# One more tile of lead for the weight parts in the up projection of a hybrid decoder trunk

## The chip, the core and the metric

The kernel runs on one core of a Trainium2 chip. The metric is device time in microseconds (us) of one execution of the whole program. TensorE (PE in the profile, PEld for its weight loads), VectorE (DVE), ScalarE (ACT), GpSimd (POOL) and SyncE (SP, which here only issues DMAs) each run their own instruction list in order and wait for one another by semaphores.

## The reference, cut to what matters

The reference is one layer of a decoder trunk on 256 rows of width 2048 in float32: an RMSNorm, a combined input projection, two token mixers, an output projection, a residual, and then a gated MLP. Only the MLP's first product is touched by the change:

```python
h = rmsnorm(x, norm_ffn_w[l])
gate, up = jnp.split(jnp.einsum('bsd,df->bsf', h, w_up[l]), 2, axis=-1)
gate = causal_dwconv(gate, conv_ffn_w[l]) + conv_ffn_b[l]
x = x + jnp.einsum('bsf,fd->bsd', jax.nn.gelu(gate, approximate=False) * up, w_down[l])
```

`w_up` is 2048 x 11264 (gate and up, 5632 columns each), so the product is 256 x 2048 by 2048 x 11264.

## The kernel before, in words

**Weights come as tiles.** The whole program walks through one list of weight tiles, `srcs`, each 256 rows x 512 columns of a matrix, held in SBUF as 128 partitions x 2 x 512 float32 (512 KB). For each tile three steps are made before TensorE uses it: a DMA into a buffer with the tag `raw` (`load_part`, L203); on ACT a cast of it to the rounded type float32r, the high part `whi` (L289); on DVE the difference of the two, the low part `wlo` (L297, called the split here). TensorE then multiplies high by high, high by low and low by high. `begin(n)` (L277) asks for cast and split of all tiles up to n; `weights()` (L197) is called once for each tile just before its matmuls and calls `begin(taken + AHEAD + 1)` with AHEAD = 2. So while tile n is multiplied, the cast and split of tile n+2 are asked for. `raw` has four buffers; `whi` and `wlo` have three each (the pool's `bufs=3`, L62). A cast of tile n therefore waits until TensorE has made its last use of the high part of tile n-3, a split until it has used up the low part of tile n-3, and a load of a raw tile until the split of the raw tile four places back is done.

**The up projection goes in groups.** There are 11 groups c = 0 to 10 of 512 gate and 512 up columns. Most of the depth of a group is done "plain": one tile, twelve matmuls of 512 columns. For a part of it the kernel uses a scheme with seven products in place of eight. The depth of 2048 is cut into four chunks of 512; a chunk treated so gives seven "parts", named T1, 11, T2, 21, T3, 22, T4, each with six matmuls. Groups 1 to 7 and 9 (`TWO`, L96) treat two chunks, 1 and 0, so they have 14 parts and 8 plain tiles; groups 8 and 10 treat one. The parts of group c+1 are put between and behind the last plain tiles of group c, so that a stretch from one group to the next is: four gate tiles and one up tile in a row, then T1, up, 11, up, T1, 11, up, and then ten parts in a row (T2, T2, 21, 21, T3, T3, 22, 22, T4, T4), with the transposes of the finished gate ahead of T3 and those of the finished up ahead of T4. `up_steps` (L100 to L127) lists this, and the PE instructions keep that order exactly (`manual_schedule`, L1446).

**Parts need sums.** A chunk's four raw quarters are loaded by `quad_load` (L218) into buffers `quad` that belong to other tags (`xt0` to `xt3`, `hhi6` to `hlo9`). Three of the seven parts are quarters themselves; the four T parts are made on DVE by subtraction in place (`up_sum`, L225, profile line L230): T1 = 12 - 11, T2 = 22 - T1 and so on, so a buffer gets its next sum only after the part in it has been cast and split. `sums_behind` says behind which tile's split each sum is put; the first T1 of a group is asked for in the main loop at `n - 3 == i` (L1482), three steps ahead of the entry that marks where the parts begin. The quarters are asked for 5 to 13 steps ahead of that entry (L1478).

**Beside the weights**, DVE also adds two pairs of products in PSUM per group (L1396, L1410), and for the group just finished makes the causal convolution (eight instructions, L1331), the product of gate and up (L1344) and the low part of the result (L1352). ACT does their activations (L1326, L1335), copies out of PSUM (L1403, L1407, L1424, L1427) and the cast L1351.

**The order on the other engines.** Outside the lists fixed by hand, a planner orders each engine's instructions: what is traced earlier in the program has the higher priority, and among the ready ones (by the planner's own estimate of times) the first is taken. On the chip each engine then runs its list in that order. `issue_after` puts an instruction behind another of its engine. The SP list holds all weight and quarter loads of this stage.

The tag `s` of the pool `fp` is a single buffer of 128 x 1024 float32; it holds sums of activations at the start of the stage (`four_sums`, L1279) and again from group 10 on.

Of the kernel before, what the change touches and what calls it, by code (L numbers as in the profile page):

```python
# [35 lines left out]
def kernel(  # L36
# [32 lines left out]
    def nm(s):  # L69
        cnt[0] += 1  # L70
        return f"{s}_{cnt[0]}"
# [30 lines left out]
    for c in range(NUP):  # L102
        kps = [kp for kp in range(KD // 2) if kp // 2 not in chunks_of[c]]
        gate_steps, up_only = ([("plain", c, col, kp) for kp in kps] for col in range(2))
        tail = min(6, len(kps)) if c + 1 in TWO else TAIL
        up_steps += gate_steps[:tail]
        for a, b in zip(gate_steps[tail:], up_only):
            up_steps += [a, b]
        rest = up_only[-tail:]
        if c + 1 == NUP:  # L110
            up_steps += rest
            break
        parts = [[("part", c + 1, what, ch) for what in UP_PARTS] for ch in chunks_of[c + 1]]
        if len(rest) == 4:
            up_steps += [rest.pop(0)]
        up_steps += [("loads", c + 1)]
        if c + 1 in TWO:
            first_four = [parts[ch][n] for ch in range(2) for n in (0, 1)] + [parts[ch][2] for ch in range(2)]
            if len(rest) == 3:
                rest = rest[:2] + [None] + rest[2:] + [None, None]  # L120
            for a, b in zip(first_four, rest):
                up_steps += [a, b] if b else [a]
            p21, t3, p22, t4 = ([parts[ch][n] for ch in range(2)] for n in range(3, 7))
            up_steps += p21 + [("gate", c)] + t3 + p22 + [("up", c)] + t4
        else:
            t1, p11, t2, p21, t3, p22, t4 = parts[0]
            up_steps += [t1, rest[0], p11, rest[1], t2, rest[2], p21, ("gate", c), t3, p22, ("up", c), t4]  # L127
    for step in up_steps:
        if step[0] == "plain":
            srcs.append(up_w[step[1]][step[2]][step[3]])  # L130
        elif step[0] == "part":
            srcs.append(("up", *step[1:]))
# [55 lines left out]
    made = []  # L188
    taken = [0]

    loads = []
    last_load = [None]
    last_split = [None]
# [2 lines left out]

    def weights(ahead=AHEAD):  # L197

        begin(taken[0] + ahead + 1)
        taken[0] += 1  # L200
        return made[taken[0] - 1]

    def load_part(n, k):  # L203
        if n == len(loads):
            if isinstance(srcs[n], tuple):
                loads.append(quarter(*srcs[n]))
                return
            loads.append(wpool.tile(list(srcs[n].shape), F32, tag="raw", name=nm("raw"), bufs=4))
        last_load[0] = nc.sync.dma_start(loads[n][:, k], srcs[n][:, k]).ins

    quarters = {}
# [65 lines left out]
    def begin(n):  # L277
        while len(made) < min(len(srcs), n):
            load(len(made) + 1)
            raw = loads[len(made)]  # L280
            if isinstance(raw, tuple):
                raw, plus, minus = raw
                nc.vector.tensor_tensor(raw, plus, minus, op=ALU.subtract)
            src = srcs[len(made)]
            shape = list(raw.shape)
            keep = kept.get(len(made))
            hi = wpool.tile(shape, F32R, tag="whi", name=nm("whi")) if keep is None else \
                mtile(keep, shape, F32R, nm("khi"))
            nc.scalar.copy(hi, raw)  # L289
            if shape[1] == 8:  # L290
                lo = None
                nc.vector.tensor_tensor(hi[:, :, 32:64], raw[:, :, 0:32], hi[:, :, 0:32].bitcast(F32),
                                        op=ALU.subtract)
            else:
                lo = wpool.tile(shape, F32R, tag="wlo", name=nm("wlo")) if keep is None else \
                    mtile(4 + keep, shape, F32R, nm("klo"))
                last_split[0] = nc.vector.tensor_tensor(lo, raw, hi.bitcast(F32), op=ALU.subtract).ins  # L297
                splits.append(last_split[0])
            made.append((hi, lo))
            for more in sums_behind.get(len(made) - 1, ()):  # L300
                up_sum(*more)
            if isinstance(src, tuple) and src[0] != "up" and src[2] in ("T1", "T3", "T2", "T4"):
                next_quarter()
# [94 lines left out]
    def mtile(i, shape, dt, name):  # L398
        return big.tile(shape, dt, tag=f"m{i}", name=name)
# [1047 lines left out]
    for i, step in enumerate(up_steps):  # L1447
# [28 lines left out]
        for n, step in enumerate(up_steps):  # L1476
            if step[0] == "loads":
                when = (7, 7, 6, 5, 13, 12, 11, 10) if step[1] in TWO else (8, 7, 6, 5)  # L1478
                for q in sorted(range(len(when)), key=lambda q: -when[q]):
                    if max(n - when[q], 0) == i:  # L1480
                        quad_load(step[1], q)
                if n - 3 == i:  # L1482
                    up_sum(step[1], "T1", chunks_of[step[1]][0])
    pe_order.close()

# [192 lines left out]
```

## Time and profile before

| what | value |
|---|---|
| median of three runs | 1541.56 us (1541.18 to 1541.80) |
| the profiled execution: its own time, and its span from first to last instruction | 1542.63 us, 1540.8 us |
| PE busy over the span | 1526.0 us (99%) |
| DVE, ACT busy over the span | 1253.4 us (81%), 849.8 us (55%) |
| first and last matmul of the up projection's tiles | 819 us, 1299 us after the span's start |
| granted TensorE clock | 0.999 |

A row of a timeline or a group has start (or count), duration, engine, the line in the kernel, the operation, and output<-inputs; in square brackets stands how long the engine had been idle before it and what released it. A row of the waits has the total, the number of waits and the longest. A row of windows has the length of the stretch and each engine's busy time in it, with the number of instructions in brackets.

### The profile page before, as it was taken

What the parts mean: (1) busy time and instruction counts of PE and PEld (TensorE: products, weight loads), DVE (VectorE), ACT (ScalarE), POOL (GpSimd) and SP (SyncE); (2) the same over time, 40 slices, a digit from 0 to 9 for tenths busy, and PEclk for the clock granted to TensorE, in tenths of its full rate; (3) what the DMA queues carried; (4) which work ended last, traced back from release to release, by engine and by line L of the source; (5) the groups of instructions that cost most, each with busy time, mean ns of one, the idle gap of its engine ahead of it and who ended that gap; (6) DMA issues with size and microseconds to landing.
All of it is one profiled execution on the core that took longest, in us unless ns stands there. A gap on an engine that the chain in (4) does not pass through costs nothing.

```text
span 1540.8 us, 20209 instructions
## 1 busy us (share of the span) xinstructions
PE 1526.0 (99%) x7302; PEld 1257.4 (82%) x7302; DVE 1253.4 (81%) x1776; ACT 849.8 (55%) x1063; POOL 70.8 (5%) x90
## 2 busy tenths in 40 slices
PE   9999999999999999999999999999999999999998
PEld 8887888788878888788888888888788888888886
DVE  6788859896589858987667899999999886878885
ACT  7455446454455445454455676666667665555552
POOL 1010002000100000000000000000000000000100
PEclk9999999999999999999999999999999999999999
DMA  8776757776577766776578646666457467556652
GB/s 276 215 221 199 202 163 214 213 214 183 152 245 205 205 169 201 222 200 186 179 250 300 194 163 217 219 205 205 150 155 242 125 216 267 183 193 205 227 189 90
DMA packets 166674, 310.46 MB, mean 201 GB/s; under 512 B 19458, under 2 KB 23330, under 8 KB 166446
## 3 DMA queue, kind: packets, MB, share of 16 engines
q1 hardware_dynamic: 159456, 287.37, 60.0%
q0 software_dynamic: 5184, 18.88, 3.7%
q10 hardware_dynamic: 1934, 2.93, 0.5%
q8 instruction: 57, 0.93, 0.2%
q14 instruction: 43, 0.35, 0.1%
HBM read 301.75 MB, written 7.38 MB: 201 GB/s over the span
## 4 chain that ended last, share of the span: by engine, by line
PE 92%; DVE 4%; issue 2%; DMA 1%; ACT 0%; POOL 0%; POOLq 0%; DVEq 0%; ACTq 0%
PE psg L1374 25%; PE psm L334 15%; PE psm L332 14%; PE psm L333 14%; PE psm L1359 7%; PE psg L1359 7%; DVE wlo L297 3%; PE psm L1374 2%; PE psm L478 1%; PE psg L377 1%; DVE quad L230 1%; PE psm L1436 1%; DMA vrow<-ev 1%; PE psg L868 1%; DMA mv<-vrow 1%
## 5 line engine op out<-in xcount | busy, mean ns | idle before, releaser
L289 ACT CAST whi<-raw 128x1024 fp32r<-128x1024 f32 x428 | 450.0, 1052 | 428.4 <-PE psm L333 280.2
L297 DVE TENSOR_TENSOR wlo<-raw,whi 128x1024 fp32r<-128x1024 f32 x426 | 517.3, 1220 | 151.2 <-ACT whi L289 146.2
L289 ACT CAST whi<-quad 128x1024 fp32r<-128x1024 f32 x168 | 176.1, 1054 | 141.0 <-DVE quad L230 39.4
L297 DVE TENSOR_TENSOR wlo<-quad,whi 128x1024 fp32r<-128x1024 f32 x168 | 202.6, 1219 | 36.2 <-ACT whi L289 35.3
L334 PE MATMUL psm<-wlo,xhl 128*128 128x512 f32 x432 | 169.5, 393 | 1.6 <-DVE wlo L297 1.6
L332 PE MATMUL psm<-whi,xhl 128*128 128x512 f32 x432 | 169.0, 391 | 0.0
L333 PE MATMUL psm<-whi,xhl 128*128 128x512 f32 x432 | 168.6, 390 | 0.0
L1374 PE MATMUL psg<-whi,fhl 128*128 128x512 f32 x504 | 127.1, 389 | 0.0
L1374 PEld LDWEIGHTS psg<-whi,fhl 128*128 128x128 f32 x504 | 94.4, 188 | 19.5
L334 PEld LDWEIGHTS psm<-wlo,xhl 128*128 128x128 f32 x432 | 81.1, 188 | 19.0 <-DVE wlo L297 2.4
L333 PEld LDWEIGHTS psm<-whi,xhl 128*128 128x128 f32 x432 | 81.1, 188 | 16.8
L332 PEld LDWEIGHTS psm<-whi,xhl 128*128 128x128 f32 x432 | 81.1, 188 | 16.6
L230 DVE TENSOR_TENSOR quad<-quad,quad 128x1024 f32<-128x1024 f32 x72 | 87.6, 1217 | 0.0
L1374 PE MATMUL psg<-wlo,fhl 128*128 128x512 f32 x252 | 69.9, 389 | 0.0
L1374 PE MATMUL psg<-whi,ups 128*128 128x512 f32 x216 | 58.9, 394 | 0.0
L1359 PE MATMUL psm<-whi,hhi 128*128 128x512 f32 (+1 forms) x150 | 58.1, 387 | 0.0
L1359 PE MATMUL psm<-whi,hlo 128*128 128x512 f32 (+1 forms) x150 | 57.9, 386 | 0.0
L1359 PE MATMUL psm<-wlo,hhi 128*128 128x512 f32 (+1 forms) x150 | 57.4, 387 | 0.1
L1374 PEld LDWEIGHTS psg<-wlo,fhl 128*128 128x128 f32 x252 | 47.3, 188 | 9.8
L332 PE MATMUL psm<-whi,mhi 128*128 128x512 f32 x128 | 50.8, 397 | 0.0
L1359 PE MATMUL psg<-whi,hhi 128*128 128x512 f32 (+1 forms) x130 | 50.3, 387 | 0.4 <-ACT whi L289 0.4
L1359 PE MATMUL psg<-whi,hlo 128*128 128x512 f32 (+1 forms) x130 | 50.0, 386 | 0.0
(432 smaller groups left out, 2927.3 us busy)
## 6 DMA issues: line engine op xcount, KB each, us to landing
raw<-in_w_in_dram SPq DMA_DIRECT2D x224, 512.0 KB, 4.2
raw<-in_w_up_dram SPq DMA_DIRECT2D x104, 512.0 KB, 4.8
quad<-in_w_up_dram SPq DMA_DIRECT2D x72, 512.0 KB, 4.9
raw<-in_w_down_dram SPq DMA_DIRECT2D x64, 512.0 KB, 4.7
raw<-in_w_out_dram SPq DMA_DIRECT2D x32, 512.0 KB, 4.2
quad<-in_w_down_dram POOLq DMA_DIRECT2D x24, 512.0 KB, 5.5
mv<-vrow SPq DMA_DIRECT2D x12, 512.0 KB, 4.9
taps<-in_conv_qkv_w_dram SPq DMA_DIRECT2D x16, 256.0 KB, 6.8
```

The source lines that it names most:

```text
L230: nc.vector.tensor_tensor(out_, plus_, minus_, op=ALU.subtract)
L289: nc.scalar.copy(hi, raw)
L297: last_split[0] = nc.vector.tensor_tensor(lo, raw, hi.bitcast(F32), op=ALU.subtract).ins
L332: mm(ps[:, t, :], lh(k, t), hi[:, kk, :], start=(k == 0), stop=False)
L333: mm(ps[:, t, :], ll(k, t), hi[:, kk, :], start=False, stop=False)
L334: mm(ps[:, t, :], lh(k, t), lo[:, kk, :], start=False, stop=(k == nk - 1))
L377: nc.tensor.transpose(pt[:, ff, t * P : (t + 1) * P], src[:, t, f * P : (f + 1) * P], ident)
L478: mm(ps_k0[:, t, :], part(k, t), w[:, kk, :], start=(k == 0 and w is hi and part is xh), stop=(k == KD - 1 and w is lo))
L868: mm(pg0, kq[:, h, 0, 0:P], kq[:, h, :, :], start=True, stop=True)
L1359: mm(ps[:, cs], lhs(kk), part_[:, kk, cs], start=(first and kk == 0 and n == 0), stop=(last and kk == 1 and n == 2), skip_group_check=shared)
L1374: mm(ps, lhs(kk), w[n][:, kk], start=(first and n == 0 and kk == 0 and lhs is high), stop=False, skip_group_check=True)
L1436: nc.tensor.transpose(out_[f // 2][:, f % 2, t * P : (t + 1) * P], e[:, t, f * P : (f + 1) * P], ident)
```

## The change

From the first part of group 1 to the last part of group 9 (the "deep" stretch, tiles 10 to 202 of the up projection, counted from 0) each tile's cast and split are asked for three tiles ahead instead of two. For this, every fourth tile of the stretch gets its high part in a new buffer `spare` and its low part in the buffer with tag `s`; the other three of four keep using the three `whi` and `wlo` buffers, which now come round every fourth tile. `spare` is what was the fourth `raw` buffer: `raw` has three buffers now, and outside the stretch every fourth raw tile is loaded into `spare`, so there are four again there. The first T1 sum of a group is asked for one step earlier for groups up to 9. Nothing is computed differently, and no instruction is added or removed.

```diff
+    deep = [0, 0]
     for step in up_steps:
+        if step[0] == "part" and not deep[0]:
+            deep[0] = len(srcs)
+        if step[0] == "part" and step[1] < NUP - 1:
+            deep[1] = len(srcs) + 1
...
+    plain_loads = [0]
...
     def weights(ahead=AHEAD):

-        begin(taken[0] + ahead + 1)
+        begin(taken[0] + ahead + (2 if deep[0] <= taken[0] + ahead + 1 < deep[1] else 1))
...
-            loads.append(wpool.tile(list(srcs[n].shape), F32, tag="raw", name=nm("raw"), bufs=4))
+            spare = not deep[0] <= n < deep[1] and plain_loads[0] % 4 == 3
+            loads.append(wpool.tile(list(srcs[n].shape), F32, tag="spare" if spare else "raw", name=nm("raw"),
+                                    bufs=1 if spare else 3))
+            plain_loads[0] += 1
+            if deep[0] <= n + 1 < deep[1]:
+                plain_loads[0] = 0
...
-            hi = wpool.tile(shape, F32R, tag="whi", name=nm("whi")) if keep is None else \
-                mtile(keep, shape, F32R, nm("khi"))
+            fourth = deep[0] <= len(made) < deep[1] and (len(made) - deep[0]) % 4 == 3
+            if fourth:
+                hi = wpool.tile(shape, F32R, tag="spare", name=nm("whi"), bufs=1)
+            else:
+                hi = wpool.tile(shape, F32R, tag="whi", name=nm("whi")) if keep is None else \
+                    mtile(keep, shape, F32R, nm("khi"))
...
-                lo = wpool.tile(shape, F32R, tag="wlo", name=nm("wlo")) if keep is None else \
-                    mtile(4 + keep, shape, F32R, nm("klo"))
+                if fourth:
+                    lo = fp.tile(shape, F32R, tag="s", name=nm("wlo"))
+                else:
+                    lo = wpool.tile(shape, F32R, tag="wlo", name=nm("wlo")) if keep is None else \
+                        mtile(4 + keep, shape, F32R, nm("klo"))
...
-                if n - 3 == i:
+                if n - (4 if step[1] < NUP - 1 else 3) == i:
                     up_sum(step[1], "T1", chunks_of[step[1]][0])
```

## The prediction

> **What bounds the kernel now.** I read the page first, then the waits of PE and PEld, then the windows from one stall to the next, and last the timelines around a stall. The page's first line, then the waits of PE and of PEld over the up projection (819 to 1300 us):
>
> ```profile
> PE 1526.0 (99%) x7302; PEld 1257.4 (82%) x7302; DVE 1253.4 (81%) x1776; ACT 849.8 (55%) x1063; POOL 70.8 (5%) x90
> ...
> PE psg L1374 <- DVE wlo L297: 4.0, 7, 0.6
> ...
> PEld psg L1374 <- DVE wlo L297: 7.1, 8, 1.1
> ```
>
> TensorE bounds the kernel, and in the up projection it waits for one thing only: seven times for a low part. The timelines of PE, then DVE, then ACT, around the last of the seven:
>
> ```profile
> 1129.11 1.07 PE L1374 MATMUL psg<-wlo,fhl 128*128 128x512 f32 x4
> 1130.02 1.07 PE L1374 MATMUL psg<-whi,ups 128*128 128x512 f32 x4
> ...
> 1135.01 0.63 PE L1374 MATMUL psg<-wlo,fhl 128*128 128x512 f32 x2
> ...
> 1139.08 1.07 PE L1374 MATMUL psg<-whi,ups 128*128 128x512 f32 x4
> 1139.99 0.63 PE L1374 MATMUL psg<-wlo,ups 128*128 128x512 f32 x2
> 1140.46 1.08 PE L1374 MATMUL psg<-whi,ups 128*128 128x512 f32 x4
> 1142.14 0.73 PE L1374 MATMUL psg<-wlo,ups 128*128 128x512 f32 x2 [0.60 <-DVE wlo L297]
> ```
> ```profile
> 1132.31 1.23 DVE L297 TENSOR_TENSOR wlo<-quad,whi 128x1024 fp32r<-128x1024 f32 x1 [0.57 <-ACT whi L289]
> 1133.45 1.22 DVE L230 TENSOR_TENSOR quad<-quad,quad 128x1024 f32<-128x1024 f32 x1
> 1134.59 0.69 DVE L1396 TENSOR_TENSOR psg<-psg,own 128x512 f32<-128x512 f32 x1
> ...
> 1140.87 1.21 DVE L297 TENSOR_TENSOR wlo<-quad,whi 128x1024 fp32r<-128x1024 f32 x1
> ```
> ```profile
> 1130.27 1.06 ACT L1427 COPY e<-psg 128x512 f32<-128x512 f32 x2
> 1131.22 1.06 ACT L289 CAST whi<-quad 128x1024 fp32r<-128x1024 f32 x1
> ```
>
> The stall is at the second "22", the eighth of the ten parts in a row. An undisturbed part goes from its first high matmul to its first low one in 0.91 us (1139.08 to 1139.99); here it takes 1.68 us (1140.46 to 1142.14), and the two low matmuls 0.73 instead of 0.63. So a stall costs 0.77 + 0.1 = 0.87 us, and all seven some 6.1 us. That is the most that can be won.
>
> Why it comes: the split that starts at 1132.31 belongs to the second "21", and TensorE takes its low part at 1135.01, 1.47 us after the split's end (1133.54). From there DVE needs 8.54 us to the end of the late split (1140.87 + 1.21 = 1142.08): four splits, three sums, one addition. TensorE, unstalled, needs 6.36 us (1135.01 to 1140.46 + 0.91). 1.47 + 6.36 - 8.54 = -0.71: the lead at the second "21" is too small by that. It is small because the cast at 1131.22 has the buffer of the first T2, whose high part TensorE uses until 1131.1 (1130.02 + 1.07); DVE stands idle for 0.57 us. So the lead of two tiles caps DVE here.
>
> But not in every group. Windows from stall to stall, and the DVE waits of the second of these windows, where none is that of a cast that waits for TensorE:
>
> ```profile
> 880.40:923.93 43.53, 42.94 (x198) 35.31 (x196) 40.37 (x42) 31.34 (x36) 0.00 (x0) 1.00 0.51 169
> 923.93:967.43 43.50, 42.88 (x197) 35.30 (x197) 41.18 (x44) 29.35 (x34) 0.00 (x0) 1.00 0.57 193
> 967.43:1010.95 43.52, 42.88 (x197) 35.30 (x197) 41.20 (x44) 29.36 (x34) 0.00 (x0) 1.00 0.59 194
> 1010.95:1054.47 43.52, 42.94 (x197) 35.34 (x197) 41.29 (x44) 29.47 (x34) 0.00 (x0) 1.00 0.57 193
> 1054.47:1098.64 44.17, 43.22 (x196) 35.23 (x196) 41.16 (x44) 29.33 (x34) 0.00 (x0) 1.00 0.57 191
> 1098.64:1142.14 43.50, 42.90 (x197) 35.31 (x197) 41.26 (x44) 29.48 (x34) 0.00 (x0) 1.00 0.50 157
> ```
> ```profile
> DVE wlo L297 <- ACT whi L289: 1.8, 2, 1.5
> DVE hlo L1352 <- ACT hhi L1351: 0.4, 1, 0.4
> ```
>
> The first number is the length, the fourth DVE's busy time. DVE works 41.2 of 43.5 us; TensorE without its stall needs 43.5 - 0.87 = 42.6. So DVE may idle 1.4 us per window before it holds TensorE up, however long the lead, and it idles 2.3. Where that comes from, in the third window (SP, ACT, DVE):
>
> ```profile
> 972.19 0.37 SPq L209 DMA_DIRECT2D raw<-in_w_up_dram  x1
> ```
> ```profile
> 977.70 1.05 ACT L289 CAST whi<-raw 128x1024 fp32r<-128x1024 f32 x1 [1.89 <-DMA raw<-in_w_up_dram]
> 978.66 0.56 ACT L1326 ACTIVATE y<-psm,vec,cfw 128x256 f32<-128x256 f32 x1
> ```
> ```profile
> 970.94 2.35 DVE L297 TENSOR_TENSOR wlo<-raw,whi 128x1024 fp32r<-128x1024 f32 x2
> 973.21 0.48 DVE L1331 SCALAR_TENSOR_TENSOR y<-psm,cfw,y 128x255 f32<-128x255 f32 x1
> 973.61 1.21 DVE L297 TENSOR_TENSOR wlo<-raw,whi 128x1024 fp32r<-128x1024 f32 x1
> 974.74 0.47 DVE L1331 SCALAR_TENSOR_TENSOR y<-psm,cfw,y 128x254 f32<-128x254 f32 x1
> 975.13 1.21 DVE L297 TENSOR_TENSOR wlo<-raw,whi 128x1024 fp32r<-128x1024 f32 x1
> 976.26 0.99 DVE L1331 SCALAR_TENSOR_TENSOR y<-psm,cfw,y 128x255 f32<-128x255 f32 x2
> 978.78 1.22 DVE L297 TENSOR_TENSOR wlo<-raw,whi 128x1024 fp32r<-128x1024 f32 x1 [1.53 <-ACT whi L289]
> ...
> 981.06 0.99 DVE L1331 SCALAR_TENSOR_TENSOR y<-psm,cfw,y 128x255 f32<-128x255 f32 x2
> 982.34 1.22 DVE L297 TENSOR_TENSOR wlo<-quad,whi 128x1024 fp32r<-128x1024 f32 x1 [0.29 <-ACT whi L289]
> ```
>
> This is the run of five plain tiles; the splits at 970.94 (two), 973.61, 975.13 and 978.78 are theirs. The fifth tile needs the raw buffer of the first: its load goes out at 972.19, when the first split ends, the cast starts at 977.70, the split at 978.78. That chain is 6.6 us long; DVE fills 5.1 of it with three splits and four convolution steps and idles 1.53.
>
> **The change part by part.** *Casts, splits, sums, matmuls and loads* keep their number and length: no instruction is added, so nothing is paid in busy time.
>
> *Lead of three tiles.* The cast of the second "21" then needs the buffer of the last plain tile instead of that of the first T2. TensorE passes from its high to its low part at 1129.11 rather than 1131.1, 2.0 us sooner. The lead there may be 3.5 us, and 1.47 + 2.0 + 6.36 - 8.54 = +1.3: no stall where DVE has the time. Whether it has is a matter of its idle time per window. With the idle of now DVE lags by the window's length less 42.6; where the cap itself makes DVE idle, 0.57 us in the sixth window and 0.61 in the fourth (row below), that goes off. Windows two to six give 0.9, 0.9, 0.4, 1.6 and 0.3, together 4.1. The first has DVE busy for only 40.4, so it ends with the full surplus of 1.3 instead of a stall, which pays for most of the next. 4.1 - 1.3 = 2.8 us of 6.1 stay: the lead alone is worth -3.3 us.
>
> ```profile
> 1044.64 1.23 DVE L297 TENSOR_TENSOR wlo<-quad,whi 128x1024 fp32r<-128x1024 f32 x1 [0.61 <-ACT whi L289]
> ```
>
> *Three raw buffers instead of four.* Inside the stretch the fourth plain tile of the run now needs the first one's buffer; the fifth needs the second's. The chain of 6.6 us from first split to refilled split stays, but one split fewer lies in it, so it has 1.13 us (2.35 for two less 1.22 for one) less to hide it, and every window's DVE time grows by that unless other work moves in. What can: in the new order a split comes one tile earlier against the convolution steps, so the two steps at 981.06 and two that now stand ahead of 970.94 may fall into the gap:
>
> ```profile
> 967.89 0.47 DVE L1331 SCALAR_TENSOR_TENSOR y<-psm,cfw,y 128x255 f32<-128x255 f32 x1
> ...
> 970.55 0.47 DVE L1331 SCALAR_TENSOR_TENSOR y<-psm,cfw,y 128x254 f32<-128x254 f32 x1
> ```
>
> Lower bound of the change in DVE's idle per window: all four come in (4 x 0.48 = 1.9 us) and the gap shrinks, 1.13 - 1.9 = -0.8. Upper bound: the activation for a later step (L1326, as at 978.66) stands behind the waiting cast on ACT's list, so that the pair at 976.26 drops out too: 1.13 + 0.99 = +2.1. I take +0.5: the row of now shows ACT's cast ahead of the next activation, so not all steps can move in, but steps that fall behind it can still cover the 0.29 us at 982.34 and the 0.4 us wait for L1351. Over windows two to six: 5 x 0.5 = +2.5 us. In the first window DVE has time to spare, so there it costs nothing.
>
> *Quarters and the T1 sum.* The sum moves with its tile: it stood behind the split asked for one step before and still does, so its distance to the tiles is unchanged. The quarter loads are not moved, so they have one step less; the longest wait of SP's list shows that they are held by sums, not by their place:
>
> ```profile
> SPq L223 <- DVE quad L230: 68.9, 6, 14.3
> ```
>
> The loads queued behind them on SP are those of the next plain run. Three of these now go ahead of the quarters as four do today; the fourth lies behind, but its buffer is free only after the run's first split, which comes later than the last quarter's. I price this at nothing; if a sum were late, the load would move with it, one for one. POOL's queue has no instruction of this stretch. *The PSUM additions* L1396 and L1410 fall one split (1.14 us) later on DVE; L1396 is finished at 1135.28 and used by the first "22" at 1139.08, so it is covered; L1410 is used by T4 and may hold it by about 0.4 us, but that replaces lag, it is not added to it; left at zero.
>
> *Sum:* -3.3 + 2.5 = -0.8 us. The profiled execution took 1542.63 us (span 1540.8), 1.07 above the median; its stalls are those of any run, so the difference is put on the median: 1541.56 - 0.8 = 1540.8.
>
> **The rivals.** *All stalls go* (faster). The convolution steps fill the gap (idle -0.5 or better per window): 2.8 - 2.5 or less remains, so 5.8 to 6.1 us are won: 1535.5 to 1535.8; with the idle unchanged 3.3, 1538.3. For it speaks that DVE is only 0.9 us per window from it; against it the ACT order. The Trainium skill (Perfetto Trace Analysis, Identifying Performance Opportunities) says that the same gap repeating on the engine that should be saturated can mean too little SBUF for the next tile. By that rule the repeated stall should go wholly with the added buffers, 1541.56 - 6.1 = 1535.5. The trace agrees in the last window (0.57 us on a buffer), but the larger repeated gap, 1.53 us, is also one of a buffer, a raw one, and there the change takes one away.
>
> *The raw buffer decides* (slower). The gap grows by 1.13 to 2.1 us in windows two to six: 2.8 + 5.7 to 10.5 remains, 2.4 to 7.2 us more than today's 6.1: 1544.0 to 1548.8. It decides from a growth of (6.1 - 2.8) / 5 = 0.7 us per window on. For it: the chain of 6.6 us is fixed by the load, 5.5 us from issue to cast. Against it: six or seven short DVE steps wait for a place.
>
> *The lead does nothing*, since DVE lags anyway and the gap does not grow: 1541.6, no change. The idle on a buffer in two of six windows speaks against it; it is the upper edge of the forecast's cases.
>
> **How the numbers follow.** The measurement tells about 0.2%, 3 us, from no change. Forecast, growth of 0 to 0.7 us, time 1538.3 to 1541.6: 0.42. All stalls go, or nearly: 0.28. Raw decides: 0.30, of which 0.05 stays within 3 us. Of the forecast's cases those near 1538.3 give 0.04 to faster. So faster 0.32, within 0.2% 0.38 + 0.05 = 0.43, slower 0.25. The forecast's own range is 1538.3 to 1541.6; the range over the cases is 1535 to 1547: it takes in the whole of the first rival and leaves out the upper end of the second and what lies beyond it.
>
> **What would show it.** In the trace after: casts of the parts no longer end their wait by a part two places back; the wait of DVE for the cast of the fourth tile of the plain run, released by a raw load, is there in each window (some 2 us, where the fifth tile's 1.53 was); PE's seven waits for L297 shrink in the first two windows most. If DVE's idle per window falls under 1.4 us, the first rival holds; if it goes over 3, the second. Wrong would be the whole reading if the stalls moved to another engine's work, the PSUM additions above all.

## The result, and the profile after

| | before | after |
|---|---|---|
| median (and range), us | 1541.68 (1540.14 to 1543.54, 8 runs) | 1546.12 (1544.21 to 1547.48, 8 runs) |
| profiled execution and its span, us | 1542.63, 1540.8 | 1545.6, 1543.9 |
| up projection, first to last matmul start, us | 479.26 | 483.24 |

The ratio is 1.0028, with a 95% interval of 1.0019 to 1.0037: the change costs 4.4 us, where 0.8 us of gain was forecast. The up projection alone is longer by 3.98 us. (One execution of `lead_four_raw`, below, took 3143 us, twice its others, and is left out of its ratio.) Busy times are as they were. The page of the changed kernel:

```profile
span 1543.9 us, 20172 instructions
...
PE 1527.0 (99%) x7302; PEld 1257.8 (81%) x7302; DVE 1253.2 (81%) x1776; ACT 846.7 (55%) x1063; POOL 70.8 (5%) x90
```

The edit adds lines, so the places have new numbers: cast L304, split L315, quarter sum L241, matmul L1392, convolution step L1349 and its activation L1344, PSUM additions L1414 and L1428, copy L1425. The waits of PE in the up projection (total, number, longest):

```profile
PE psg L1392 <- DVE wlo L315: 3.7, 7, 1.1
PE psg L1392 <- DVE psg L1414: 0.7, 1, 0.7
PE psg L1392 <- ACT psg L1425: 0.7, 1, 0.7
PE psm L1392 <- DVE ups L1304: 0.6, 1, 0.6
PE psg L1392 <- DVE psg L1428: 0.2, 1, 0.2
```

The change was made to do away with the first row, and that row still has seven waits (4.0 us before). Four other waits are new. Counted from the matmuls' starts, before has seven places where a start comes more than 0.45 us after the one ahead of it, and they lose 5.1 us against the usual 0.226 us; after has twelve, and they lose 7.9. One of the new ones, 0.8 us at the first T1 of group 1 behind the sums of activations (`ups`, L1304), stands in every kernel below that asks three tiles ahead and in none that asks two.

The old stall sat at the second "22" of groups 2 to 7 (the seventh at the first "22" of group 6). The largest new ones sit one pair earlier, at the second T3. PE, DVE and ACT around that of group 5 (start, duration, engine, line, operation; in brackets the idle time before):

```profile
1050.59 1.07 PE L1392 MATMUL psg<-whi,ups 128*128 128x512 f32 x4
1052.78 0.73 PE L1392 MATMUL psg<-wlo,ups 128*128 128x512 f32 x2 [1.12 <-DVE wlo L315]
```
```profile
1048.10 2.35 DVE L315 TENSOR_TENSOR wlo<-quad,whi 128x1024 fp32r<-128x1024 f32 x2
1050.37 1.22 DVE L241 TENSOR_TENSOR quad<-quad,quad 128x1024 f32<-128x1024 f32 x1
1051.50 1.22 DVE L315 TENSOR_TENSOR wlo<-quad,whi 128x1024 fp32r<-128x1024 f32 x1
1052.64 1.22 DVE L241 TENSOR_TENSOR quad<-quad,quad 128x1024 f32<-128x1024 f32 x1
```

The second split at 1048.10 is not that of the next tile: it is the split of the first "22" (tile 114, counted from 0 along the up projection), put ahead of that of the second T3 (tile 113), which then starts at 1051.50 and holds TensorE up. In the lists of the changed kernel eleven neighbouring pairs of tiles have changed places on DVE, and none had before. Two pairs in groups 3, 5 and 7 each stand at the two stalls of the group, which lose 4.5 us together.

And the raw tiles come late. ACT and DVE in the run of five plain tiles of the same window:

```profile
1019.78 1.05 ACT L304 CAST whi<-raw 128x1024 fp32r<-128x1024 f32 x1 [2.93 <-DMA raw<-in_w_up_dram]
...
1022.86 1.05 ACT L304 CAST whi<-raw 128x1024 fp32r<-128x1024 f32 x1 [1.56 <-DMA raw<-in_w_up_dram]
```
```profile
1020.86 1.23 DVE L315 TENSOR_TENSOR wlo<-raw,whi 128x1024 fp32r<-128x1024 f32 x1 [1.43 <-ACT whi L304]
...
1023.95 1.22 DVE L315 TENSOR_TENSOR wlo<-raw,whi 128x1024 fp32r<-128x1024 f32 x1 [0.95 <-ACT whi L304]
```

The prediction expected one gap of some 2 us there; there are two, of 2.4 us together. So the profile offers three culprits: the order, the raw buffer, and asking further ahead. The runs take them apart.

### The profile page after: what moved, and what is told of

It reads as the page before. It is cut to its first block, busy times and chain, and to the rows that moved or that the text cites. A ratio compares the mean times of both kernels' runs of the same rounds, so it can differ in the third digit from the quotient of the medians.

```text
span 1543.9 us, 20172 instructions
## 1 busy us (share of the span) xinstructions
PE 1527.0 (99%) x7302; PEld 1257.8 (81%) x7302; DVE 1253.2 (81%) x1776; ACT 846.7 (55%) x1063; POOL 70.8 (5%) x90
## 5 line engine op out<-in xcount | busy, mean ns | idle before, releaser
L304 ACT CAST whi<-raw 128x1024 fp32r<-128x1024 f32 x428 | 449.6, 1052 | 435.2 <-PE psm L351 281.5
L315 DVE TENSOR_TENSOR wlo<-raw,whi 128x1024 fp32r<-128x1024 f32 x426 | 517.6, 1221 | 162.0 <-ACT whi L304 156.9
L304 ACT CAST whi<-quad 128x1024 fp32r<-128x1024 f32 x168 | 174.4, 1052 | 131.2 <-PE psg L1392 32.4
L315 DVE TENSOR_TENSOR wlo<-quad,whi 128x1024 fp32r<-128x1024 f32 x168 | 202.9, 1221 | 29.7 <-ACT whi L304 28.5
L1392 PE MATMUL psg<-whi,fhl 128*128 128x512 f32 x504 | 127.2, 390 | 0.0
L1392 PEld LDWEIGHTS psg<-whi,fhl 128*128 128x128 f32 x504 | 94.5, 188 | 19.6
L241 DVE TENSOR_TENSOR quad<-quad,quad 128x1024 f32<-128x1024 f32 x72 | 87.8, 1219 | 0.0
L1392 PE MATMUL psg<-wlo,fhl 128*128 128x512 f32 x252 | 69.9, 390 | 0.0
L1392 PE MATMUL psg<-whi,ups 128*128 128x512 f32 x216 | 59.1, 395 | 1.4 <-DVE psg L1414 0.7
L1392 PEld LDWEIGHTS psg<-wlo,fhl 128*128 128x128 f32 x252 | 47.3, 188 | 9.9
```

Of the source, the lines that this page charges most:

```text
L241: nc.vector.tensor_tensor(out_, plus_, minus_, op=ALU.subtract)
L1392: mm(ps, lhs(kk), w[n][:, kk], start=(first and n == 0 and kk == 0 and lhs is high), stop=False, skip_group_check=True)
```

## The experiments

Each was timed beside the kernel before (4 to 11 executions each; medians of before 1540.7 to 1542.4 us). A "home" is a pair of buffers, one for a high and one for a low part. "Loss" is what TensorE loses at starts over 0.45 us apart in the up projection, as above.

| kernel | homes | raw buffers | asked ahead | order | ratio to before (95%) | up, us | loss, us (places) |
|---|---|---|---|---|---|---|---|
| before | 3 | 4 | 2 | planner | 1 | 479.3 | 5.1 (7) |
| the change | 4 | 3 | 3 | planner | 1.0028 (1.0019 to 1.0037) | 483.2 | 7.9 (12) |
| raw_three | 3 | 3 | 2 | planner | 1.0105 (1.0092 to 1.0119) | 497.1 | 17.6 (13) |
| order_kept | 4 | 3 | 3 | tiles kept | 1.0045 (1.0032 to 1.0059) | 485.4 | 9.5 (13) |
| lead_four_raw | 4 | 4 | 3 | planner | 1.0160 (1.0146 to 1.0175) | 503.8 | 21.3 (8) |
| lead_four_raw_order | 4 | 4 | 3 | tiles kept | 1.0167 (1.0153 to 1.0181) | 504.0 | 21.7 (8) |
| homes_three_raw | 4 | 3 | 2 | planner | 1.0098 (1.0084 to 1.0112) | 494.0 | 14.9 (6) |
| homes_four_raw_conv | 4 | 4 | 2 | T1's split tied | 1.0040 (1.0027 to 1.0052) | 485.8 | 8.9 (7) |
| homes_four_raw_conv_order | 4 | 4 | 2 | tied, tiles kept | 1.0106 (1.0092 to 1.0120) | 494.4 | 15.6 (27) |
| homes_three_raw_conv_order | 4 | 3 | 2 | tied, tiles kept | 1.0108 (1.0092 to 1.0123) | 494.7 | 14.8 (24) |
| homes_four_raw_steps | 4 | 4 | 2 | held | **0.9966 (0.9952 to 0.9979)** | 473.9 | 0.4 (1) |
| homes_three_raw_steps | 4 | 3 | 2 | held | 1.0017 (1.0008 to 1.0025) | 481.4 | 6.2 (12) |
| change_steps | 4 | 3 | 3 | held | 0.9999 (0.9990 to 1.0008) | 479.0 | 4.1 (7) |
| raw_three_steps | 3 | 3 | 2 | held | 1.0063 (1.0049 to 1.0077) | 490.2 | 12.2 (22) |
| less_dve | 3 | 4 | 2 | planner | 0.9998 (0.9989 to 1.0007) | 478.8 | 4.6 (6) |

### First set: the raw buffer, the order and the lead apart

The first theory was that the exchanged pairs of tiles (A), the raw buffer (B) or both make the loss. `raw_three` takes only the fourth raw buffer away. `order_kept` is the change with casts and splits tied in the order of the tiles. `lead_four_raw` is the change without the loss of the raw buffer: the fourth high part goes into buffers that are empty until group 5 and group 7 are finished, so the stretch ends with group 7. `lead_four_raw_order` has both. All kernels below with four homes and four raw buffers have these homes and this shorter stretch.

```diff
 raw_three (against before)
-  ... tag="raw", name=nm("raw"), bufs=4))
+  ... tag="spare" if spare else "raw", name=nm("raw"), bufs=1 if spare else 3))
 order_kept (against the change)
-            nc.scalar.copy(hi, raw)
+            with tc.issue_after(last_cast[0]) if up_tile and last_cast[0] is not None else ExitStack():
+                last_cast[0] = nc.scalar.copy(hi, raw).ins
...
+                with tc.issue_after(last_split[0]) if up_tile and last_split[0] is not None else ExitStack():
 lead_four_raw (against the change)
+  ... tag="raw", name=nm("raw"), bufs=4))
-                hi = wpool.tile(shape, F32R, tag="spare", name=nm("whi"), bufs=1)
+                hi = fp.tile(shape, F32R, tag="hlo5" if len(made) < deep[2] else "hlo7", name=nm("whi"))
```

> Three raw buffers instead of four inside the stretch, and nothing else: lead of two tiles, three high and three low buffers, first T1 sum where it was; the buffer spare stays idle there. Theory A (order: the loss comes from casts and splits that the planner put out of the order of the tiles, 70 before 69 and 73 before 72 in group 3, and the same in groups 5 and 7): here no pair is out of order, so the loss is what the longer gap before the fourth plain tile costs alone, 0 to 2 us (up to 0.13% slower). Theory B (raw: the third buffer less is the loss): the gap grows by 1.13 us in five windows and nothing pays it back, 4 to 6 us slower (0.26 to 0.39%), as much as the whole change lost or more.

> The changed kernel, with each cast of the stretch put behind the cast of the tile before it on ACT's list and each split behind the split before it on DVE's. Theory A: the six stalls that follow a swapped pair (at 964.9, 970.4, 1052.8, 1058.3, 1141.4 and 1146.9 us in the changed kernel's trace, 4.5 us together beyond the 0.23 us from one matmul to the next) go or shrink to 0.3 us each, 3 us are won against the changed kernel, and it stands 1 to 1.5 us above the kernel before (0.1%). Theory B: the order costs nothing, since DVE's time per window is what counts, and the time is that of the changed kernel, 4.4 us above the kernel before (0.28%).

> The lead of three tiles with all four raw buffers kept. The fourth high part goes into a buffer that is idle at that time (the tag hlo5 up to the last part of group 6, hlo7 through group 7); the stretch ends with group 7's parts. The planner's lists have no split out of order and two casts, both where the stretch or its home changes. Both theories expect a gain on the kernel before: theory B, and the prediction's own sum without its raw term, 3.3 us (0.2% faster), theory A the same or up to 6.1 us (0.4%). If it is not faster, the lead has no worth and the sum was wrong in its first term.

> As lead_four_raw, with each cast behind the cast before and each split behind the split before, as in order_kept. Its order differs from lead_four_raw only in the two casts, so both theories expect the time of lead_four_raw within 1 us; what it tells is whether holding the order costs anything by itself. Against order_kept it has the fourth raw buffer more: theory B expects it 4 us faster than order_kept or more, theory A 0 to 2 us beyond what the lead itself brings.

None of the four came out as expected. Keeping the tiles in order made the change slower (1549.5 us): the stalls at the second T3 and at T4 go, but nine come back at the "22" of groups 3 to 7, and the T3 of group 8 waits longer for its PSUM addition. So the exchanged pairs by themselves aren't what the change loses by. `order_kept`, waits of PE (L1396 the matmul, L319 the split, L1418 the addition):

```profile
PE psg L1396 <- DVE wlo L319: 4.9, 10, 0.6
PE psg L1396 <- DVE psg L1418: 1.5, 1, 1.5
```

`raw_three` lost 16 us and `lead_four_raw`, which was to win, lost 24. The waits of PE in the up projection show a row that neither kernel of the case has; first `lead_four_raw` (its L1389 is the matmul, L1346 the convolution step), then `raw_three`:

```profile
PE psm L1389 <- DVE y L1346: 18.9, 5, 4.4
PE psm L1389 <- DVE ups L1301: 0.7, 1, 0.7
```
```profile
PE psm L1392 <- DVE y L1349: 11.6, 6, 3.2
PE psg L1392 <- DVE wlo L315: 3.7, 6, 0.6
```

With four homes and four raw buffers no matmul waits for a low part any more, while `raw_three`, which also waits at T1, still has six such waits. But a group's first T1 takes its PSUM buffer from a pool of two (tag `psm`), and the one that it gets held the transposes of the finished gate. It is free when the last of eight convolution steps on DVE has read it. In `lead_four_raw`, PE and DVE around the T1 of group 4:

```profile
989.45 1.07 PE L1389 MATMUL psg<-wlo,fhl2a 128*128 128x512 f32 x4
994.20 1.15 PE L1389 MATMUL psm<-whi,ups 128*128 128x512 f32 x4 [3.68 <-DVE y L1346]
```
```profile
988.65 1.22 DVE L312 TENSOR_TENSOR wlo<-quad,whi 128x1024 fp32r<-128x1024 f32 x1
989.78 1.22 DVE L238 TENSOR_TENSOR quad<-quad,quad 128x1024 f32<-128x1024 f32 x1
990.91 0.48 DVE L1346 SCALAR_TENSOR_TENSOR y<-psm,cfw,y 128x255 f32<-128x255 f32 x1
991.31 1.22 DVE L312 TENSOR_TENSOR wlo<-raw,whi 128x1024 fp32r<-128x1024 f32 x1
992.44 1.22 DVE L238 TENSOR_TENSOR quad<-quad,quad 128x1024 f32<-128x1024 f32 x1
993.58 0.48 DVE L1346 SCALAR_TENSOR_TENSOR y<-psm,cfw,y 128x254 f32<-128x254 f32 x1
```

TensorE is ready for T1 at 990.5 and waits until 994.0: the last two steps stand behind a sum, a split and another sum. The lists of DVE say the same without times. A number is the split of that tile (79 is that first T1), c a convolution step, Y the product of gate and up:

```
before                [71] add c [72] [73] c [74] [75] c [76] c [77] c c [78] sum c c [79] Y [80]
the change            [71] add c [73] [72] [74] c [75] [76] c c [77] c c [78] sum c c [79] [80] Y
raw_three             [71] add c [72] [73] c [74] [75] c [76] c [77] c [78] sum c [79] c [80] c [81] sum Y
order_kept            [71] add c [72] [73] [74] c [75] [76] c c [77] c c [78] sum c c [79] [80] [81] sum Y
lead_four_raw         [71] [72] add c [73] [74] [75] c [76] [77] c [78] sum c [79] c [80] c [81] sum c [82] sum c Y
homes_three_raw       [71] [72] add c [73] [74] [75] c [76] c c [77] c [78] sum c [79] [80] c [81] sum c [82] sum Y
homes_four_raw_steps  [71] add c [72] [73] [74] c [75] c c [76] [77] c c [78] sum c c [79] Y [80]
change_steps          [71] add [72] c [73] [74] c [75] c c [76] c c [77] c c [78] sum Y [79] [80]
```

So the second theory: the size of a buffer ring moves the planner's list, and the last convolution step moves behind later splits (H). The planner takes the first ready instruction; with a home more, a split is ready whenever a step still waits; the list of `raw_three` changes without a home more, and why isn't shown. That this is how the steps sink is argued from the lists; that they sink, and that T1 then waits for them, is what the rows show.

### Second set: homes alone, and T1's wait tied away

`homes_three_raw` is the change with tiles asked for as far ahead as before. In the other three T1's split is tied behind the last convolution step, so that the splits can't pass it.

```diff
 homes_three_raw (against the change)
-        begin(taken[0] + ahead + (2 if deep[0] <= taken[0] + ahead + 1 < deep[1] else 1))
+        begin(taken[0] + ahead + 1)
...
-                if n - (4 if step[1] < NUP - 1 else 3) == i:
+                if n - 3 == i:
 the three others
+                first_t1 = isinstance(src, tuple) and src[0] == "up" and src[2] == "T1" and src[3] == chunks_of[src[1]][0]
+                behind = last_conv[0] if first_t1 else last_ups[0] if len(made) == deep[0] + 1 else None
+                with tc.issue_after(behind) if behind is not None else ExitStack():
```

> The change's four homes and three raw buffers, but each cast and split asked for as far ahead as before. Theory H (it is the homes that cost: with one more home the planner may put splits and sums ahead of the convolution steps, and a group's first T1 matmul then waits for the last step that reads its PSUM buffer): the last step that frees that buffer comes two sums later than before, so T1 is held 2 to 4 us in groups three to eight as with three raw buffers alone (11.6 us in six waits there), and matmuls after it run at half rate; 8 to 20 us slower than before. Theory Q (asking one tile further ahead is what cost the change its 4.4 us): as before, within 1 us.

> Four homes, all four raw buffers, asked for as before; casts and splits kept in tile order, T1's first split behind the last convolution step that reads the PSUM buffer, so that T1 cannot be held by it. Theory L (the lead is worth what the prediction said, once the convolution steps are in place): no wait of matmuls for low parts (3.6 us in six waits and seven stalls of 0.73 to 1.03 us before), no wait of T1: 3.3 to 6.1 us faster than before. Theory D (the stalls are VectorE's own shortage inside a window, which no number of homes makes good): the stalls move to the splits behind the five steps in a row; within 1.5 us of before or slower.

> The same with three raw buffers, as in the change. Theory L with the prediction's raw price: 2 to 6 us slower than with four raw buffers, from waits of ScalarE's casts for raw tiles (before: a few tenths per window). If raw buffers cost nothing by themselves: within 1 us of the one with four.

> Four homes, four raw buffers, asked for as before, T1's first split behind the last convolution step, casts and splits left to the planner (several pairs change places). If T1's wait is all that four homes cost: 3 to 6 us faster than before. If tiles out of order cost on their own: 1 to 4 us slower than the one kept in order.

`homes_three_raw` came out as theory H had it, 15 us slower than before, by this one wait of PE in the up projection:

```profile
PE psm L1392 <- DVE y L1349: 13.9, 6, 3.1
```

So it is not the asking ahead that costs. On the contrary: with the same buffers the change, which asks one tile further ahead, is 10 us faster than this (1546.1 against 1556.3), because its list has the last step where before has it, ahead of [79], while that of `homes_three_raw` has it behind [81] and a sum.

The tie didn't settle it. With it T1's wait is small, but in `homes_four_raw_conv_order` DVE now waits for the activation that opens each block of the convolution, and these waits turn into 27 small stalls. DVE's waits in six windows (881 to 1144 us), L1355 being the step and L1350 the activation on ACT:

```profile
DVE y L1355 <- ACT y L1350: 14.7, 10, 2.2
```

On ACT the casts have gone ahead of the activations in the same way as splits ahead of steps. A tie on DVE alone makes DVE wait for an ACT that is late; nothing was learned here about the lead. Its twin with three raw buffers, `homes_three_raw_conv_order`, took the same time (1557.2 us against 1557.3): the raw buffer's price doesn't show where TensorE is held up by something else. `homes_four_raw_conv`, without the tile order, is 10.5 us faster than the one that keeps it, against expectation, and still waits 3.7 us at a single T1:

```profile
PE psm L1395 <- DVE y L1351: 3.7, 1, 3.7
```

### Third set: the order of before, held

In these the activations on ACT and the steps on DVE are tied ahead of the casts and splits that followed them in before, casts and splits in the order of the tiles, and the second tile of the stretch behind the activation sums. Put on the kernel before, the same hold leaves the list of every engine exactly as it is, so a difference comes from the buffers and the asking. But the hold binds one way only: a step can't fall behind, it can still move forward, and with other buffers the planner does move some (last two rows of the lists above). So what a buffer is worth here includes these moves.

```diff
+            near = [k for k in (-4, -3, -2, -1, 0, 1) if len(made) - k in first_t1] if step_convs else []
+            near = near[0] if near else None
+            cast_behind = {-3: 1, -2: 1, -1: 2, 0: 3, 1: 4}.get(near)
+            split_behind = {-4: 1, -3: 2, -2: 3, -1: 5, 0: 7}.get(near)
+            after_cast = last_cast[0] if deep[0] <= len(made) < deep[1] else None
+            with tc.issue_after(step_acts[cast_behind]) if cast_behind is not None else ExitStack(), \
+                    tc.issue_after(after_cast) if after_cast is not None else ExitStack():
+                last_cast[0] = nc.scalar.copy(hi, raw).ins
...
+                behind = step_convs[split_behind] if split_behind is not None else \
+                    last_ups[0] if len(made) == deep[0] + 1 else None
...
 less_dve (against before)
-                for j in (1, 0):
+                for j in (1, 0) if c == NUP - 1 or f not in (1, 3) else (1,):
```

> Four homes and all four raw buffers, asked for as before; the planner is held to the order of before: the activations of the gate's convolution on ScalarE ahead of the same casts, its steps on VectorE ahead of the same splits, casts and splits in tile order. So the lead stands alone. Theory L (a longer lead removes the waits for low parts, as the prediction had it, and only the convolution's place spoiled it): seven stalls gone or nearly, 3 to 6 us faster than before. Theory D (TensorE's stalls are VectorE's own shortage, which no number of homes makes good): about as many microseconds of stalls as before, within 1.5 us of it.

> The same held order with three raw buffers, which sets apart the price of the raw buffer. The prediction's size: 2.5 us slower than with four. If the loads come early enough with three: within 0.5 us.

> The change whole, asked for one tile further ahead, with the same held order. If the change's 4.4 us came from the places that the planner gave to convolution steps, casts and splits: at or below before (-3 to 0 us). If asking further ahead with three raw buffers costs on its own: 2 to 5 us slower than before.

> Before, with less work on VectorE: the gate's convolution leaves out one of its two steps for two of four blocks (0.95 us of 41.2 us per window); three homes, order else as before. Theory H (the stall at the second 22 is the homes' cap, whatever VectorE has to spare): the six stalls of 0.73 to 1.03 us stay, time within 1 us of before. Theory D (VectorE's shortage sets them): the stalls of groups three to seven shrink by what is saved, 3 to 5 us faster.

> Three raw buffers and the three homes of before, asked for as before, in the held order: the raw buffer's price without the lead. If lead and raw buffer add up: 8 us slower than before (1543.6 less 1535.6 with four homes). If three raw buffers cost only where casts run further ahead and so want their raw tiles earlier: 0 to 3 us, near the prediction's 2.5.

`homes_four_raw_steps` is the fourth home alone, through group 7 and asked for two tiles ahead as before, and it is the fastest kernel of the study: 1535.62 us (1534.6 to 1537.9), 5.5 us under before and 10.5 under the change. The seven stalls are gone; PE's waits in the up projection are this one row, and in two windows that held a stall each PE is busy without a break (columns: length, then the busy time of PE, its weight loads, DVE, ACT and POOL, the granted clock, DMA share, GB/s):

```profile
PE psg L1409 <- DVE wlo L329: 0.2, 1, 0.2
```
```profile
923.60:967.10 43.50, 43.50 (x201) 36.20 (x200) 41.45 (x45) 29.04 (x34) 0.00 (x0) 1.00 0.57 199
967.10:1010.60 43.50, 43.50 (x201) 36.20 (x200) 42.16 (x44) 29.06 (x34) 0.00 (x0) 1.00 0.59 202
```

From the first T1 of one group to that of the next it takes 42.60 us in each of the five steps from group 2 to group 7, the time that the prediction gave TensorE without its stall; before took 43.5, and once 44.2. Mean busy times over these five (length 42.60):

```profile
sum 213.00, PE 213.00 PEld 177.25 DVE 206.31 ACT 146.32 POOL 0.00; mean PE 42.60 PEld 35.45 DVE 41.26 ACT 29.26 POOL 0.00
```

`less_dve` says the same from the other side. It leaves out two convolution steps per group. With 0.95 us less for DVE to do per window, six of the seven stalls stay at their size (PE's waits, L1374 being the matmul and L297 the split), and the time doesn't move. DVE spends what it saves on waiting for casts; the second row is for 881 to 1144 us, where before has 12.6 us:

```profile
PE psg L1374 <- DVE wlo L297: 3.6, 6, 0.6
...
DVE wlo L297 <- ACT whi L289: 16.8, 21, 1.8
```

So less work for DVE doesn't take the stalls away and a home more does, with DVE's work unchanged: the homes made them, not DVE's shortage (theory D).

With three raw buffers in the same order (`homes_three_raw_steps`) the time is 8.0 us longer than with four (1543.62 against 1535.62). DVE's and ACT's waits from 881 to 1144 us, with four raw buffers (cast L313, split L329) and then with three (L316, L332):

```profile
ACT whi L313 <- DMA raw<-in_w_up_dram: 8.3, 5, 2.0
DVE wlo L329 <- ACT whi L313: 7.5, 17, 1.0
```
```profile
ACT whi L316 <- DMA raw<-in_w_up_dram: 14.8, 10, 3.7
DVE wlo L332 <- ACT whi L316: 14.6, 15, 3.1
PE psg L1412 <- ACT psg L1445: 1.7, 3, 0.7
```

ACT's wait for raw tiles grows by 6.5 us and DVE's wait for casts by 7.1. Part of it reaches PE through ACT's copy of a PSUM bank (L1445), which stands behind a late cast. `raw_three_steps`, three homes and three raw buffers, is 9.7 us slower than before by the ratio, 10.9 between the medians. So the raw buffer costs some 8 to 11 us, with the fourth home or without it. The pair with four homes isn't quite alike: with four raw buffers the stretch ends with group 7, and 1.3 us of the difference in the profiled executions lies in the step from group 8 to 9 (37.49 us from T1 to T1 against 36.19).

`change_steps` is the change in the held order: as before (0.9999). Against `homes_three_raw_steps` it asks one tile further ahead and is 2.35 us faster for it; against the change itself it is better by the order alone, 4.5 us by the ratios. Tile order isn't what it wins by: `order_kept` has its casts and splits in the order of the tiles too and stands at 1.0045. What the two differ in is the place of the convolution: in `change_steps` all eight steps stand ahead of [78], in `order_kept` the last two behind it, as in before (lists above).

## Why the prediction was wrong

The account, between medians of one set: four homes −5.5 us, the raw buffer +8.0, asking further ahead −2.35, together +0.1 (the change in the held order). The planner's own order instead of the held one then adds 1.0028 less 0.9999, 0.29% or 4.5 us, and 4.4 were measured. The prediction had −3.3 for homes and asking together, +2.5 for the raw buffer, and nothing for the order. The split between homes and raw buffer depends on which comes first: with the raw buffer taken away first (`raw_three_steps`) it is +10.9, and the homes are then worth −8.4.

The step that lost the sign is "in the new order a split comes one tile earlier against the convolution steps": the prediction moved before's list by one place, where the planner made a new one, which costs 4.5 us. With the order held, the time (1541.27) lies within the forecast's range. That would have been luck: the terms are off by −2.2, −2.35 and +5.5 us, and the errors nearly cancel.

- **The stalls and what they are worth.** Right: they can all go. Of the 6.1 us set as the most that can be won, the fourth home alone won 5.5. (In the prediction's sum the fourth window's 0.4 is 0.3 by its own figures, 43.52 less 42.6 less 0.61; this changes nothing.)
- **"Lead of three tiles", −3.3 us.** The place was right, the size too small: −5.5 for the homes alone. The failing step is "With the idle of now DVE lags". DVE may idle 1.4 us per window, as the prediction says, but the 2.3 that it idles did not stay: with four homes it is 42.60 less 41.26, 1.34 us (rows above). Over 881 to 1144 us DVE waits for casts 7.5 us, while ACT waits 8.3 for raw tiles. Before had, in the same stretch:

```profile
DVE wlo L297 <- ACT whi L289: 12.6, 18, 2.2
ACT whi L289 <- DMA raw<-in_w_up_dram: 8.8, 5, 2.6
```

  So ACT's raw wait stayed and DVE's fell by 5.1. How, the run of five plain tiles shows, ACT's cast and then DVE's steps and fifth split in `homes_four_raw_steps`, the same tiles as in the prediction's third window:

```profile
973.27 1.05 ACT L313 CAST whi<-raw 128x1024 fp32r<-128x1024 f32 x1 [1.81 <-DMA raw<-in_w_up_dram]
```
```profile
968.02 0.48 DVE L1365 SCALAR_TENSOR_TENSOR y<-psm,cfw,y 128x254 f32<-128x254 f32 x1
...
969.55 1.00 DVE L1365 SCALAR_TENSOR_TENSOR y<-psm,cfw,y 128x255 f32<-128x255 f32 x2
...
972.73 0.99 DVE L1365 SCALAR_TENSOR_TENSOR y<-psm,cfw,y 128x255 f32<-128x255 f32 x2
974.35 1.23 DVE L329 TENSOR_TENSOR wlo<-raw,whi 128x1024 fp32r<-128x1024 f32 x1 [0.62 <-ACT whi L313]
```

  ACT waits for the raw tile as long as before (1.89), but five steps stand between the first and the fifth split where before has four, and DVE idles 0.62 us in place of 1.53. That is the mechanism of the rival "all stalls go", convolution steps that fill the gap, and its time (1535.5) is what this kernel took (1535.6).
- **"Three raw buffers instead of four", +2.5 us.** The place was right, the size was not: +8.0 to +10.9. The prediction let the convolution steps fill part of the longer gap and took 0.5 us per window; DVE's extra wait is 7.1 / 6 = 1.2 us per window, near the 1.13 of one split fewer under the chain of 6.6 us before anything is filled in. The filling was the wrong choice within its own bounds (−0.8 to 2.1): behind the first plain split the list has five steps in the gap with three raw buffers as with four, so nothing more moved in. Beyond that, ACT is late for its PSUM copies, which no step had priced.
- **The order.** No step priced it. In the planner's own lists eleven pairs are exchanged and casts and splits stand ahead of convolution steps; by `order_kept` the pairs are not what costs. The order costs the change 4.5 us against the held one, and it cost 13 us (`homes_three_raw` against `homes_three_raw_steps`, 1556.3 and 1543.6) with one asking step less.
- **The rivals.** "The raw buffer decides" named 1544.0 to 1548.8 us, and the time is there. Its mechanism is half of the truth: its price of 5.7 to 10.5 us holds 8.0, but the larger worth of the homes and the asking balances it, and with the order held the change stands where before does (0.9999).
- **What would show it wrong.** The prediction named the PSUM additions. One stall each at L1414 and L1428 and one at ACT's copy L1425 did appear, 1.6 us in all: true, but the smaller part.

The rule cited there from the Trainium skill (Perfetto Trace Analysis, section Identifying Performance Opportunities), that the same gap repeating on the engine that should be saturated can mean too few buffers, agrees with this case: a fourth home, with the planner's moves held in check, brought the loss at the seven gaps from 5.1 us to 0.4.

Not settled: what a fourth home through group 9 would be worth with all four raw buffers, or asked for three tiles ahead in the held order, since no run has either; why asking further ahead gives the planner so much better a list in the change than in `homes_three_raw`, and whether the order can be held more cheaply than by tying each step.

## What to carry to other kernels

A buffer added to a ring also changes the order that a list scheduler makes, since instructions that used to be blocked become ready and go ahead of work that only filled gaps; compare each engine's list before and after, and see who frees the next PSUM bank. When buffers are moved from one ring to another, price the ring that loses by the time of one refill chain not covered, and don't count on other work to move into the gap. Here a fourth home with the loads' ring left whole and the convolution held in place won 5.5 us, where the change lost 4.4.

## What the hardware showed beside that

After some of the long waits for a PSUM buffer TensorE ran at half rate for a while. The windows behind the T1 of group 3 in `lead_four_raw`, and behind those of group 3 and group 4 in `homes_three_raw` (columns: length, busy time of PE, granted clock, DMA share, GB/s):

```profile
945.30:950.80 5.50, 5.50 (x14) 0.50 0.15 60
```
```profile
942.20:946.70 4.50, 4.50 (x14) 0.64 1.02 375
989.40:993.90 4.50, 4.50 (x20) 1.00 0.90 321
```

The slow matmuls start 0.427 us apart instead of 0.22, and the granted clock of these windows is 0.50 and 0.64, against 1.00 in the third, which has none. The waits ahead of these windows, in the same order:

```profile
944.74 0.76 PE L1389 MATMUL psm<-whi,ups 128*128 128x512 f32 x1 [4.16 <-DVE y L1346]
```
```profile
942.13 1.15 PE L1392 MATMUL psm<-whi,ups 128*128 128x512 f32 x4 [2.12 <-DVE y L1349]
...
989.34 0.93 PE L1392 MATMUL psm<-whi,ups 128*128 128x512 f32 x3 [2.71 <-DVE y L1349]
```

A wait of 2.12 us was followed by seven slow matmuls, one of 2.71 us by none; in `raw_three` one of 1.94 us was followed by seven. So here the length of the wait alone doesn't decide. In `lead_four_raw` 42 matmuls ran slow, which adds 42 x 0.21 = 8.8 us to the 21.3 us that it loses at its long waits. The Trainium skill (TensorE: Matmul & The Clock Gate, section "Part 1: The HAM clock gate") puts this down to an activity window of about 3.4 us that runs free of the kernel; a window that begins at any moment fits waits of like length with and without slow matmuls, but half clock after a wait of 2.12 us is earlier than a whole idle window of that length would give, and here the measurement decides.
